# The opening in written order with halved first transfers, and a tail that scales the first row block last

## The chip, the cores and the metric

The kernel runs on one core of a Trainium2 chip. The metric is the time of one execution in microseconds of the device, the median of several runs; the profiled execution is one run more. A core has five engines that work side by side, each through its own list of instructions in order: TensorE (PE in the profile; its weight loads are PEld), VectorE (DVE), ScalarE (ACT), GpSimd (POOL) and SyncE (SP). SP, ACT and POOL also issue DMAs; an engine that issues one goes on at once, unless the issue itself has to wait for a semaphore, in which case all that stands behind it on this engine waits too.

## The reference

One decoder layer on 256 tokens of width 1024, all in float32:

```python
xn = rmsnorm(h, norm_mix_g[l])
q_a, k_a, v_a, q_b, f_b, i_b, og_b, g_a, g_b = split_cols(xn @ w_in[l])
y_a = moba_attention(q_a, k_a, v_a, positions) @ w_br_attn[l]
y_b = hgrn2(q_b, f_b, i_b, og_b, lb_all[l], hgrn_norm_g[l]) @ w_br_hgrn[l]
h = h + (sigmoid(g_a) * y_a + sigmoid(g_b) * y_b) @ w_out[l]
h = h + memory_cross_attention(rmsnorm(h, norm_x_g[l]), rmsnorm(mem, norm_mem_g[l]), ...)
hn = rmsnorm(h, norm_ffn_g[l])
gu = hn @ w_ffn_in[l]
h = h + (silu(gu[..., :2816]) * gu[..., 2816:]) @ w_ffn_out[l]
return rmsnorm(h, final_norm_g)
```

Two places matter here. The first is the product of the scaled input with the columns of `w_in` that give `f_b` (the scaling by the row's root mean square is applied later, to the product). The second is the last line: each of the 256 rows of `h` is squared and summed over its 1024 columns, the power -1/2 of the mean is taken, and the row is multiplied with it and with the gain `final_norm_g`.

## The kernel before

Every float32 product is made of three: both operands are split into a high part in the rounded type `float32r` (on ACT, L212, for the weights) and the rest (on DVE, L213), and PE adds high x high, high x low and low x high. The weights come as a row of chunks of 128 x 2048 elements (1 MB), in the order in which PE uses them, each into one of a few buffers `raw`, are split into `hi` and `lo`, and are used by PE. PE's instructions run in the order in which the code is written; ACT and DVE are otherwise ordered by a scheduler, which places each instruction where its own estimate of the times puts it, except in regions that are marked as written by hand. The kernel's DMAs from SP and ACT take eight completion semaphores (DMAHW0 to DMAHW7) in turn; a DMA whose semaphore is still in use by an earlier one waits at its issue until that one has landed.

*The opening* (L361 to L400, and L547 to L558 for PE). The tokens are held with features on the partitions, as 8 slices k of 128 features by 256 tokens. The gains and slice 0 of x are one DMA, `x0g` (L366, on ACT); slice 1 is the first `xraw` piece, slices 2 and 3 the second (both L384, on ACT), slices 4 to 7 the third (L384, on SP). `gv`, a table of all other gains and the positions, is the last DMA on ACT (L390). The first weight chunk comes in four pieces (L209, on SP, 512 columns of its 2048 each), one for each k of 0 to 3; the second chunk in two (L203), and so on. `part_x(k)` makes the high part `Xh` of a slice (slice 0 on DVE, L380, the others on ACT, L378) and the rest `Xl` (on DVE, L381). The loop of L391 takes for each k the DMA of the k-th weight piece, then `part_x(k)`, and then the split of that piece. PE first multiplies zeros (`warm`, L372, 15 matmuls of 256 columns), and then, for i of 0 to 8 (L548): four matmuls with slice i (Xh and Xl, two row blocks t, L553), and two with the low part of slice i - 1's weights (L558). `lx` and `le` (L469 to L471 on DVE) and what follows them are a small softmax over two of gv's columns; the rope tables on POOL read gv too (L407).

*The tail* (L1403 to L1468, ordered by hand on ACT, DVE, POOL and SP). The last product is added up in PSUM banks, by row block t of 128 tokens and column half c: `acc[t, c]`; block (1, 1) is finished in two quarters, `ends[0]` and `ends[1]`, with two banks of their own. For each finished piece `add_out` adds it to the residual H (DVE, L1425), `mean_part` squares it and sums the squares along the row (ACT, L1428), and `gain` multiplies it with the final gain (POOL, L1433), for all but the two quarters. `power` takes the power -1/2 of the summed mean (POOL, L1436). Row block 0 is then scaled and sent in the middle of this, half a row by ACT (L1450) and half by DVE (L1458); row block 1 at the end: half a row by ACT (L1463, sent from ACT), and the two quarters by DVE with gain and scale in one (L1467).

## Time and profile before

| | us |
|---|---|
| median of 3 runs (lowest, highest) | 600.08 (599.79, 600.6) |
| the profiled execution | 601.15 |
| its span, from the first to the last instruction | 599.4 |
| PE busy | 591.1 (99%) |
| DVE busy | 456.3 (76%) |
| ACT busy | 371.9 (62%) |
| POOL busy | 118.9 (20%) |
| mean granted clock of TensorE | 0.946 |

How to read it: times in a timeline count from the span's start. A row of the timeline gives the start, the length, the engine, the line of the code, the instruction, its output and inputs with their shapes, and in brackets how long the engine was idle before it and what ended this. An engine's name with a q (SPq, ACTq) is its instruction queue issuing a DMA. The busy time of PE counts matmuls that overlap as busy once; a busy PE is not a PE at its peak. Spans on POOL are rough.

### The profile page before, as it was taken

The numbers are of one execution on the slowest core, as the hardware profiler recorded it, in microseconds if no ns is written. First come the engines' busy times: TensorE is split into PE (matmuls) and PEld (weight loads), VectorE is DVE, ScalarE is ACT, GpSimd is POOL, SyncE is SP. The second block draws the span as 40 slices with busy tenths as digits, with TensorE's granted clock in tenths as the row PEclk, the third lists the DMA queues.
The fourth block names the chain that finished last, engine by engine and source line by source line (L and its number), as shares of the span: only waits on it lengthen the run. The fifth ranks groups of instructions, "written<-read, shape, count | busy, mean of one in ns | idle before, by whom it ended". The sixth has DMA issues, their size and how long they took to land.

```text
span 599.4 us, 8532 instructions
## 1 busy us (share of the span) xinstructions
PE 591.1 (99%) x3189; PEld 494.9 (83%) x3189; DVE 456.3 (76%) x743; ACT 371.9 (62%) x600; POOL 118.9 (20%) x137
## 2 busy tenths in 40 slices
PE   8999999999999999999999999999999999999995
PEld 7888888888888888788888888888888888888884
DVE  7689669999776866649966657787699887878763
ACT  7797464343487566637556556675488767676742
POOL 2889300212300440001312513100100000000003
PEclk9999999999999999999999999999999999999998
DMA  9959995874885579579699789765999979796501
GB/s 342 394 212 312 295 308 208 255 299 159 261 292 212 209 192 294 217 281 385 176 315 284 279 280 277 204 225 207 360 298 300 369 252 355 267 358 203 186 1 70
DMA packets 21833, 155.76 MB, mean 260 GB/s; under 512 B 2736, under 2 KB 3376, under 8 KB 5296
## 3 DMA queue, kind: packets, MB, share of 16 engines
q1 hardware_dynamic: 17712, 117.68, 51.3%
q0 software_dynamic: 2880, 20.97, 17.9%
q10 hardware_dynamic: 1200, 16.57, 7.2%
q8 instruction: 25, 0.41, 0.3%
q14 instruction: 16, 0.13, 0.1%
HBM read 154.16 MB, written 32.51 MB: 311 GB/s over the span
## 4 chain that ended last, share of the span: by engine, by line
PE 98%; DMA 1%; POOL 0%; DVE 0%; issue 0%; ACT 0%; POOLq 0%; DVEq 0%; ACTq 0%
PE pst L281 14%; PE pst L283 13%; PE pst L282 13%; PE psf L296 7%; PE bk L283 6%; PE bk L281 6%; PE bk L282 6%; PE psf L297 4%; PE acc L282 3%; PE acc L283 3%; PE acc L281 3%; PE psg L553 1%; PE pso L283 1%; PE pso L281 1%; PE pso L282 1%; PE lp L671 1%
## 5 line engine op out<-in xcount | busy, mean ns | idle before, releaser
L213 DVE TENSOR_TENSOR lo<-raw,hi 128x1024 fp32r<-128x1024 f32 (+1 forms) x128 | 156.0, 1238 | 47.6 <-ACT hi L212 45.6
L212 ACT ACTIVATE hi<-raw 128x1024 fp32r<-128x1024 f32 (+1 forms) x128 | 128.6, 1029 | 88.4 <-PE pst L283 45.2
L281 PE MATMUL pst<-hi,Xh 128*128 128x512 f32 x224 | 88.7, 396 | 0.0
L283 PE MATMUL pst<-hi,Xh 128*128 128x512 f32 x224 | 87.3, 390 | 0.0
L282 PE MATMUL pst<-lo,Xh 128*128 128x512 f32 x224 | 87.2, 389 | 0.0
L1219 DVE TENSOR_TENSOR lo<-raw,hi 128x1024 fp32r<-128x1024 f32 x56 | 66.1, 1220 | 13.9 <-ACT hi L1218 13.9
L1218 ACT ACTIVATE hi<-raw 128x1024 fp32r<-128x1024 f32 x56 | 56.3, 1053 | 21.4 <-issue 11.3
L281 PEld LDWEIGHTS pst<-hi,Xh 128*128 128x128 f32 x224 | 42.1, 188 | 9.1 <-issue 0.5
L283 PEld LDWEIGHTS pst<-hi,Xh 128*128 128x128 f32 x224 | 42.1, 188 | 8.9
L282 PEld LDWEIGHTS pst<-lo,Xh 128*128 128x128 f32 x224 | 42.1, 188 | 8.3
L1201 POOL DMA_DIRECT2D raw<-w x5 | 4.5, 895 | 119.3 <-DVE lo L1219 33.8
L281 PE MATMUL acc<-hi,hids 128*128 128x512 f32 x64 | 25.1, 392 | 0.0
L282 PE MATMUL acc<-lo,hids 128*128 128x512 f32 x64 | 24.9, 390 | 0.0
L283 PE MATMUL acc<-hi,hids 128*128 128x512 f32 x64 | 24.9, 389 | 0.0
L281 PE MATMUL bk<-hi,Sh 128*128 128x512 f32 x60 | 23.7, 396 | 0.0
L281 PE MATMUL bk<-hi,h2h 128*128 128x512 f32 x60 | 23.7, 394 | 0.0
L283 PE MATMUL bk<-hi,h2h 128*128 128x512 f32 x60 | 23.4, 390 | 0.0
L283 PE MATMUL bk<-hi,Sh 128*128 128x512 f32 x60 | 23.4, 390 | 0.0
L282 PE MATMUL bk<-lo,Sh 128*128 128x512 f32 x60 | 23.4, 389 | 0.0
L282 PE MATMUL bk<-lo,h2h 128*128 128x512 f32 x60 | 23.3, 389 | 0.0
L296 PE MATMUL psf<-H,hi 128*128 128x512 f32 x64 | 22.8, 400 | 0.0
L296 PE MATMUL psf<-M,hi 128*128 128x512 f32 x64 | 22.8, 399 | 0.0
(382 smaller groups left out, 1462.1 us busy)
## 6 DMA issues: line engine op xcount, KB each, us to landing
raw<-w SPq DMA_DIRECT2D x78, 1024.0 KB, 6.7
sum<-w POOLq DMA_DIRECT2D x15, 1024.0 KB, 12.4
raw<-sum SPq DMA_DIRECT2D x13, 1024.0 KB, 6.5
raws<-w SPq DMA_DIRECT2D x11, 1024.0 KB, 6.8
raw<-w POOLq DMA_DIRECT2D x5, 1024.0 KB, 8.6
raw<-w SPq DMA_DIRECT2D x4, 512.0 KB, 5.9
raws<-sum SPq DMA_DIRECT2D x2, 1024.0 KB, 5.1
raw<-w SPq DMA_DIRECT2D x4, 256.0 KB, 4.4
```

The source lines that it names most:

```text
L212: SC.activation(hi[:, a], raw[:, a], AF.Copy)
L213: V.tensor_tensor(lo[:, a], raw[:, a], hi[:, a].bitcast(F32), op=ALU.subtract)
L281: PE.matmul(ps, xh, h, start=first, stop=False, skip_group_check=more)
L282: PE.matmul(ps, xh, l, start=False, stop=False, skip_group_check=more)
L283: PE.matmul(ps, xl, h, start=False, stop=last, skip_group_check=more)
L296: PE.matmul(ps, w[0][:, k, a], X2[:, k], start=k == 0, stop=False)
L297: PE.matmul(ps[:, 0], w[1][:, k, a], X2[:, k, 0], start=False, stop=k == 7)
L553: PE.matmul(pss[c][t], z[:, k, t * 128:(t + 1) * 128], ws[c][0][:, k], start=z is Xh and k == 0, stop=False)
L671: PE.matmul(ps[r, j], KS[:, a, r], q, start=True, stop=True)
L1201: G.dma_start(raw_of[k], A["w"][AT_CHUNK["I", PAIRS[g][0], 1]], accum_op=ALU.add)
L1218: SC.activation(hi[:, a], raw[:, a], AF.Copy)
L1219: V.tensor_tensor(lo[:, a], raw[:, a], hi[:, a].bitcast(F32), op=ALU.subtract)
```

## The change

In the opening:

- `x0g` becomes two DMAs on ACT: slice 0's first 128 tokens with the gains, and its last 128 tokens. `Xh` and `Xl` of slice 0 are made in two halves.
- The first weight piece (512 columns) becomes two DMAs of 256 columns, each split for itself (`FIRST`), so the first chunk comes in five pieces.
- `gv` is issued on SP behind the first chunk's five pieces, and no longer on ACT.
- The opening's loop stands in a region ordered by hand for ACT and DVE, which ends after the second chunk's splits; slice 0's `part_x` comes before the first split.
- The zeros for the warm-up are written by one memset in place of memset and cast, ahead of the other two memsets, and PE makes 13 warm-up matmuls instead of 15.

In the tail:

- PE finishes `acc[1, 0]` before `acc[1, 1]`, and the two are added to H in this order.
- The gain of the first of the two last quarters is applied ahead on POOL (`gain(1, 1, 256)`).
- The last quarter's squares are summed by DVE in one instruction (`tensor_tensor_reduce`), which starts from the sum of the others; the first quarter's sum is added to that start by ACT (`Identity` with a bias).
- Row block 0 is scaled and sent only behind all of this, and not between the squares.

```diff
-WARM = 15
+WARM = 13
+FIRST = (0, 256, 512, 1024, 1536, 2048)
...
-        x0g = big("B4", "x0g", (128, 264))
-        SC.dma_start(x0g, A["x0g"])
-        zero, still = t2b("zero", (128, 256)), tb.tile([128, 256], F32R, name="still", tag="tb")
-        V.memset(zero, 0.0)
-        V.tensor_copy(still, zero)
+        x0g = [big(tag, "x0g", (128, n)) for tag, n in (("B4", 136), ("B6", 128))]
+        for i in range(2):
+            SC.dma_start(x0g[i], A["x0g%d" % i])
+        still = tb.tile([128, 256], F32R, name="still", tag="tb")
+        V.memset(still.bitcast(F32), 0.0)
+        V.memset(ones, 1.0)
+        V.memset(nhalf, -0.5)
...
+            token_halves = [(slice(128 * t, 128 * t + 128), x0g[t][:, 0:128]) for t in range(2)]
+            for a, xk in token_halves:
+                V.tensor_scalar(Xh[:, k, a], xk, g1, None, op0=ALU.mult)
+            for a, xk in token_halves:
+                V.scalar_tensor_tensor(Xl[:, k, a], xk, g1, Xh[:, k, a].bitcast(F32), op0=ALU.mult, op1=ALU.subtract)
...
-        SC.dma_start(gv, A["gv"])
-        for k in range(4):
+        region = tc.manual_schedule(engines={mybir.EngineType.Activation, mybir.EngineType.DVE})
+        region.__enter__()
+        next(opening[0])
+        part_x(0)
+        next(opening[0])
+        for k in range(1, 4):
             next(opening[0])
             part_x(k)
         run(opening[0])
+        SY.dma_start(gv, A["gv"])
         run(opening[1])
+        region.__exit__(None, None, None)
...
+        out_part(n, wb, 1, 0)
         out_part(n - 1, wa, 1, 1)
-        out_part(n, wb, 1, 0)
...
-        add_out(acc[1, 1], 1, 512, 1024)
-        V.tensor_scalar(v3[:, 0:1], ssq3[:, 0:1], ssq3[:, 1:2], EPS, op0=ALU.add, op1=ALU.add)
-        power(0, 0)
-        SC.activation(H[:, 0, 0:512], hg3[0, 0], AF.Copy, scale=rs[0])
-        send(SY, 0, 0, 512)
         add_out(acc[1, 0], 1, 0, 512)
         mean_part(2, 1, 0, 512)
         gain(1, 0)
...
+        V.tensor_scalar(v3[:, 0:1], ssq3[:, 0:1], ssq3[:, 1:2], EPS, op0=ALU.add, op1=ALU.add)
+        power(0, 0)
+        add_out(acc[1, 1], 1, 512, 1024)
+        V.tensor_scalar(v3[:, 1:2], ssq3[:, 2:3], EPS, None, op0=ALU.add)
+        add_out(ends[0], 1, 512, 768)
+        mean_part(3, 1, 512, 768)
+        gain(1, 1, 256)
+        SC.activation(v3[:, 2:3], ssq3[:, 3:4], AF.Identity, bias=v3[:, 1:2])
+        add_out(ends[1], 1, 768, 1024)
+        V.tensor_tensor_reduce(out=pt.tile([128, 256], F32, name="fjunk", tag="pt"), in0=H[:, 1, 768:1024],
+                               in1=H[:, 1, 768:1024], op0=ALU.mult, op1=ALU.add, scale=1.0 / 1024.0,
+                               scalar=v3[:, 2:3], accum_out=v3[:, 3:4])
+        power(1, 3)
+        SC.activation(H[:, 0, 0:512], hg3[0, 0], AF.Copy, scale=rs[0])
+        send(SY, 0, 0, 512)
         V.tensor_scalar(H[:, 0, 512:1024], hg3[0, 1], rs[0], None, op0=ALU.mult)
         send(SY, 0, 512, 1024)
...
+        V.tensor_scalar(H[:, 1, 512:768], hg3[1, 1][:, :256], rs[1], None, op0=ALU.mult)
+        send(SY, 1, 512, 768)
+        V.scalar_tensor_tensor(H[:, 1, 768:1024], H[:, 1, 768:1024], rs[1], gfin[:, 768:1024], op0=ALU.mult, op1=ALU.mult)
+        send(SY, 1, 768, 1024)
```

How the lists of the engines change is shown at three places. In the rows, 128x264 and the like are shapes, x4 is a count, and behind "waits" stand the semaphores that a row waits for. The first place is the start of ACT: before,

```order
L366 DMA x0g<-x0g 128x264
L387 ACT_TABLE_LOAD
L387 ACTIVATE warm_act<-ones 128x1 [waits DVE_49]
L384 DMA xraw<-xT 128x256
L384 DMA xraw<-xT 128x512
L390 DMA gv<-gv 128x90 [waits DMAHW0_49]
L212 ACTIVATE hi<-raw 128x512 [waits DMAHW1_49]
L378 ACTIVATE Xh<-xraw,x0g 128x256 [waits DMAHW4_49]
L212 ACTIVATE hi<-raw 128x512 [waits DMAHW2_49]
```

and now:

```order
L367 DMA x0g<-x0g 128x136
L367 DMA x0g<-x0g 128x128
L393 ACT_TABLE_LOAD
L393 ACTIVATE warm_act<-ones 128x1 [waits DVE_49]
L390 DMA xraw<-xT 128x256
L390 DMA xraw<-xT 128x512 [waits DMAHW0_49]
L212 ACTIVATE hi<-raw 128x256 [waits DMAHW1_49]
L212 ACTIVATE hi<-raw 128x256 [waits DMAHW3_49]
L380 ACTIVATE Xh<-xraw,x0g 128x256 [waits DMAHW6_49]
L212 ACTIVATE hi<-raw 128x512 [waits DMAHW4_49]
```

DMAHW0 is the semaphore of the first `x0g` DMA in both. The DMA of gv has gone; the second `xraw` DMA (slices 2 and 3) has the wait for DMAHW0 that gv had. On SP gv stands as the sixth DMA now, behind the five pieces of the first chunk, with a wait for DMAHW1 (the first of them) and ahead of the second chunk.

The second place is DVE in the opening, from `Xh` of slice 0 to `lo` of the weight piece for k = 2: before,

```order
L380 TENSOR_SCALAR Xh<-x0g 128x256 [waits DMAHW0_49]
L381 SCALAR_TENSOR_TENSOR Xh<-x0g,Xh 128x256 [waits DVE_49]
L213 TENSOR_TENSOR lo<-raw,hi 128x512 [waits DMAHW1_49,Activation_49]
L381 SCALAR_TENSOR_TENSOR Xh<-xraw,x0g,Xh 128x256 [waits DMAHW4_49,Activation_49]
L213 TENSOR_TENSOR lo<-raw,hi 128x512 [waits DMAHW2_49,Activation_49]
L381 SCALAR_TENSOR_TENSOR Xh<-xraw,x0g,Xh 128x256 [waits DMAHW6_49,Activation_49]
L213 TENSOR_TENSOR lo<-raw,hi 128x512 [waits DMAHW3_49,Activation_49]
```

and now (the tile Xh holds `Xh` and `Xl`; the rows L387 and L381 write `Xl`):

```order
L385 TENSOR_SCALAR Xh<-x0g 128x128 [waits DMAHW0_49]
L385 TENSOR_SCALAR Xh<-x0g 128x128 [waits DMAHW2_49]
L387 SCALAR_TENSOR_TENSOR Xh<-x0g,Xh 128x128 [waits DVE_49] x2
L213 TENSOR_TENSOR lo<-raw,hi 128x256 [waits DMAHW1_49,Activation_49]
L213 TENSOR_TENSOR lo<-raw,hi 128x256 [waits DMAHW3_49,Activation_49]
L381 SCALAR_TENSOR_TENSOR Xh<-xraw,x0g,Xh 128x256 [waits DMAHW6_49,Activation_49]
L481 TENSOR_TENSOR lx<-gv 128x8 [waits DMAHW1_49]
L213 TENSOR_TENSOR lo<-raw,hi 128x512 [waits DMAHW4_49,Activation_49]
L381 SCALAR_TENSOR_TENSOR Xh<-xraw,x0g,Xh 128x256 [waits DMAHW0_49,Activation_49]
L213 TENSOR_TENSOR lo<-raw,hi 128x512 [waits DMAHW5_49,Activation_49]
```

`lx`, which reads gv, stood behind the Xl of slices 4 to 7 before; now the scheduler has put it between `Xl` of slice 1 and `lo` of that slice's weights, into the order written by hand.

The third place is the end of DVE: before,

```order
L1425 TENSOR_TENSOR H<-acc,H 128x512 [waits PE_49] x3
L1448 TENSOR_SCALAR v_5340<-ssq_5336 128x1 [waits Activation_49]
L1425 TENSOR_TENSOR H<-acc,H 128x512 [waits PE_49]
L1425 TENSOR_TENSOR H<-bk,H 128x256 [waits DVE_49,PE_49]
L1425 TENSOR_TENSOR H<-bk,H 128x256 [waits PE_49]
L1458 TENSOR_SCALAR H<-hg_5338,r_f_5341 128x512 [waits Pool_49]
L1460 TENSOR_SCALAR v_5340<-ssq_5336 128x1 [waits Activation_49]
L1461 TENSOR_SCALAR v_5340<-ssq_5336,v_5340 128x1 [waits DVE_49,Activation_49]
L1467 SCALAR_TENSOR_TENSOR H<-H,r_f_5342,gfin 128x256 [waits Pool_49]
L1467 SCALAR_TENSOR_TENSOR H<-H,r_f_5342,gfin 128x256
```

and now (hg is a piece with its gain, r_f a power, v and ssq sums of squares; the two ISA rows are the sum of the last quarter's squares and its reading):

```order
L1437 TENSOR_TENSOR H<-acc,H 128x512 [waits PE_49] x3
L1462 TENSOR_SCALAR v_5347<-ssq_5342 128x1 [waits Activation_49]
L1437 TENSOR_TENSOR H<-acc,H 128x512 [waits PE_49]
L1465 TENSOR_SCALAR v_5347<-ssq_5342 128x1 [waits Activation_49]
L1437 TENSOR_TENSOR H<-bk,H 128x256 [waits DVE_49,PE_49]
L1437 TENSOR_TENSOR H<-bk,H 128x256 [waits PE_49]
L1471 ISA fjunk,v_5347<-H,v_5347 128x256 [waits DVE_49,Activation_49]
L1471 ISA v_5347 128x1
L1477 TENSOR_SCALAR H<-hg_5344,r_f_5348 128x512 [waits Pool_49]
L1481 TENSOR_SCALAR H<-hg_5346,r_f_5349 128x256 [waits Pool_49]
L1483 SCALAR_TENSOR_TENSOR H<-H,r_f_5349,gfin 128x256 [waits DVE_49]
```

One of the two small steps behind the last add has gone, the other stands ahead of the first quarter's add; the sum of squares has come behind the second quarter's, and row block 0's scaling stands behind it.

More of the change, by code (lines that the diff above doesn't have):

```diff
@@ L98, in lay @@
                 out[i].reshape(n, 128, 4 // n, 512)[...] = w.reshape(n, 4 // n, 128, 512).transpose(0, 2, 1, 3)
+                if i == 0:
+                    out[i].reshape(4, 2, 128, 256)[0] = w[:128].reshape(128, 2, 256).transpose(1, 0, 2)
             else:
@@ L175, in build @@
         ones = cp.tile([128, 1], F32, name="ones")
-        V.memset(nhalf, -0.5)
-        V.memset(ones, 1.0)
         ready = {}
@@ L198, in prep @@
             pieces = 4 if first else 2
-            n = 2048 // pieces
+            bounds = FIRST if i == 0 else tuple(range(0, 2049, 2048 // pieces))
             sent = PIECES[i] if i < len(PIECES) else 1
@@ L205, in prep @@
                 SY.dma_start(raw, A["w"][i])
-            for c in range(pieces):
-                a = slice(c * n, (c + 1) * n)
+            for a in (slice(*z) for z in zip(bounds, bounds[1:])):
                 if i == 0:
@@ L375, in part_x @@
         def part_x(k):
-            g1, xk = x0g[:, 256 + k:257 + k], xraw[:, k] if k else x0g[:, 0:256]
+            g1 = x0g[0][:, 128 + k:129 + k]
             if k:
-                SC.activation(Xh[:, k], xk, AF.Copy, scale=g1)
-            else:
-                V.tensor_scalar(Xh[:, k], xk, g1, None, op0=ALU.mult)
-            V.scalar_tensor_tensor(Xl[:, k], xk, g1, Xh[:, k].bitcast(F32), op0=ALU.mult, op1=ALU.subtract)
+                SC.activation(Xh[:, k], xraw[:, k], AF.Copy, scale=g1)
+                V.scalar_tensor_tensor(Xl[:, k], xraw[:, k], g1, Xh[:, k].bitcast(F32), op0=ALU.mult, op1=ALU.subtract)
+                return
+            token_halves = [(slice(128 * t, 128 * t + 128), x0g[t][:, 0:128]) for t in range(2)]
[3 more added lines that the diff above has]
+                V.scalar_tensor_tensor(Xl[:, k, a], xk, g1, Xh[:, k, a].bitcast(F32), op0=ALU.mult, op1=ALU.subtract)
         def take_x(eng, a, b):
@@ L1415, in build @@
             out_part(n, wb, 1, 1, ends[i], 256 * i, 256 * i + 256)
-        ssq3 = cp.tile([128, 5], F32, name="ssq3")
-        hg3 = {i: big(tag, "hg3", (128, 512)) for tag, i in (("B12", (0, 0)), ("B7", (0, 1)), ("B14", (1, 0)))}
-        v3 = cp.tile([128, 3], F32, name="v3")
+        ssq3 = cp.tile([128, 4], F32, name="ssq3")
+        hg3 = {i: big(tag, "hg3", (128, 512)) for tag, i in (("B12", (0, 0)), ("B7", (0, 1)), ("B14", (1, 0)), ("P1", (1, 1)))}
+        v3 = cp.tile([128, 4], F32, name="v3")
         rs = [cp.tile([128, 1], F32, name="r_f%d" % t) for t in range(2)]
@@ L1429, in mean_part, with gain @@
                           accum_out=ssq3[:, i:i + 1])
-        def gain(t, c):
-            a = slice(c * 512, (c + 1) * 512)
-            G.tensor_tensor(hg3[t, c], H[:, t, a], gfin[:, a], op=ALU.mult)
+        def gain(t, c, n=512):
+            a = slice(c * 512, c * 512 + n)
+            G.tensor_tensor(hg3[t, c][:, :n], H[:, t, a], gfin[:, a], op=ALU.mult)
         def power(t, i):
@@ L1454, in build @@
         gain(1, 0)
-        for i in range(2):
-            add_out(ends[i], 1, 512 + 256 * i, 768 + 256 * i)
-            mean_part(3 + i, 1, 512 + 256 * i, 768 + 256 * i)
+        V.tensor_scalar(v3[:, 0:1], ssq3[:, 0:1], ssq3[:, 1:2], EPS, op0=ALU.add, op1=ALU.add)
[13 more added lines that the diff above has]
+        send(SY, 0, 0, 512)
         V.tensor_scalar(H[:, 0, 512:1024], hg3[0, 1], rs[0], None, op0=ALU.mult)
         send(SY, 0, 512, 1024)
-        V.tensor_scalar(v3[:, 1:2], ssq3[:, 2:3], ssq3[:, 3:4], EPS, op0=ALU.add, op1=ALU.add)
-        V.tensor_scalar(v3[:, 2:3], ssq3[:, 4:5], v3[:, 1:2], None, op0=ALU.add)
-        power(1, 2)
         SC.activation(H[:, 1, 0:512], hg3[1, 0], AF.Copy, scale=rs[1])
         send(SC, 1, 0, 512)
-        for i in range(2):
-            a = slice(512 + 256 * i, 768 + 256 * i)
-            V.scalar_tensor_tensor(H[:, 1, a], H[:, 1, a], rs[1], gfin[:, a], op0=ALU.mult, op1=ALU.mult)
-            send(SY, 1, a.start, a.stop)
+        V.tensor_scalar(H[:, 1, 512:768], hg3[1, 1][:, :256], rs[1], None, op0=ALU.mult)
+        send(SY, 1, 512, 768)
+        V.scalar_tensor_tensor(H[:, 1, 768:1024], H[:, 1, 768:1024], rs[1], gfin[:, 768:1024], op0=ALU.mult, op1=ALU.mult)
+        send(SY, 1, 768, 1024)
         region.__exit__(None, None, None)
@@ L1494 @@
         "xT": by_piece(feats(a["x"])),
-        "x0g": np.ascontiguousarray(np.concatenate([feats(a["x"])[:, 0], cols(a["norm_mix_g"][0])], axis=1)),
+        "x0g0": np.ascontiguousarray(np.concatenate([feats(a["x"])[:, 0, :128], cols(a["norm_mix_g"][0])], axis=1)),
+        "x0g1": np.ascontiguousarray(feats(a["x"])[:, 0, 128:]),
         "xtok": tokens(a["x"]),
```

## The prediction

> **What bounds the kernel now.** I read the page first, then the windows of PE alone, then the two ends of the span. The span and the chain of work that ended last:
>
> ```profile
> span 599.4 us, 8532 instructions
> ...
> PE 98%; DMA 1%; POOL 0%; DVE 0%; issue 0%; ACT 0%; POOLq 0%; DVEq 0%; ACTq 0%
> ```
>
> The windows of PE (length, busy time with instructions, granted clock, DMA share, GB/s), first and last of four that lie end to end:
>
> ```profile
> 8.00:100.00 92.00, 92.00 (x546) 0.95 0.86 302
> ...
> 500.00:592.80 92.80, 92.80 (x427) 0.95 0.58 202
> ```
>
> In both PE is busy for the whole stretch. So the time is an opening until about 8 us, a block of matmuls without a gap, and a tail behind them. The change leaves the middle's order alone; whatever moves the last late start of the opening moves the end by as much. The chain in the opening (start, length):
>
> ```profile
> 0.73 3.51 DMA x0g<-x0g
> ...
> 4.26 0.34 ACTq L390
> 4.64 0.64 ACT hi L212
> 5.33 2.20 PE psg L553 x8
> ...
> 9.53 0.91 PE psg L553 x4
> ```
>
> The gain table's issue (L390) waits on ACT for x0g, and the first weight split stands behind it; the first real matmul is at 5.33, and one of 512 columns takes 0.227 (four in 0.91). But this is not yet the start that counts. The timeline of the opening (start, length, [idle before and its end]):
>
> ```profile
> 1.21 0.29 DVE L369 CAST still<-zero 128x256 fp32r<-128x256 f32 x1
> 1.25 0.86 ACTq L384 DMA_DIRECT2D xraw<-xT  x2
> ...
> 1.56 3.57 PE L372 MATMUL warm<-still 128*128 128x256 f32 x15 [1.56 <-DVE still L369]
> ...
> 2.56 1.80 SPq L203 DMA_DIRECT2D raw<-w  x2
> ...
> 6.79 0.51 ACT L378 ACTIVATE Xh<-xraw,x0g 128x256 fp32r<-128x256 f32 x1 [0.50 <-DMA xraw<-xT]
> ...
> 7.21 0.62 ACT L212 ACTIVATE hi<-raw 128x512 fp32r<-128x512 f32 x1
> 7.33 0.49 DVE L381 SCALAR_TENSOR_TENSOR Xh<-xraw,x0g,Xh 128x256 fp32r<-128x256 f32 x1 [0.32 <-ACT Xh L378]
> ...
> 7.86 0.69 DVE L213 TENSOR_TENSOR lo<-raw,hi 128x512 fp32r<-128x512 f32 x1
> ...
> 7.88 1.20 PE L553 MATMUL psg<-hi,Xh 128*128 128x512 f32 x4
> ```
>
> Ten matmuls from 5.33 would end at 7.6. The third feature slice (k=2) starts at 7.88, because its 256 KB of x land at 6.79, then Xh (to 7.30) and the split of the weights (to 7.83) follow on ACT. From 7.88 PE has no gap. **The start that counts is landing of xraw k=2,3 plus 1.09.**
>
> **The opening, part by part.** DMAs of the opening and, for comparison, one of the outputs (KB, us from issue to landing):
>
> ```profile
> xraw<-xT ACTq DMA_DIRECT2D x1, 256.0 KB, 5.1
> ...
> out<-H SPq DMA_DIRECT2D x2, 128.0 KB, 2.2
> ...
> x0g<-x0g ACTq DMA_DIRECT2D x1, 132.0 KB, 3.5
> ...
> gv<-gv ACTq DMA_DIRECT2D x1, 45.0 KB, 5.9
> ```
>
> *First transfers.* x0g becomes 68 and 64 KB, the first weights 128 and 128. Both x0g and raw's first piece (388 KB) are in by 4.24 now; of the first halves only 196 KB have to come. The bound below is 2.9 (0.73 plus the output row's 2.2 us), above 4.24. I take 3.85, nearer to the x0g row, since it has the same place in the queues. The second halves then come by about 4.5. With gv's issue gone from ACT, the two half splits (L212's 0.64 for 512 columns; about 0.4 each) end near 5.0, and the first real matmul starts about 0.3 earlier. Of this nothing reaches the end: the next slices wait for data.
>
> *The issue that now waits.* The order rows of ACT show that the wait for x0g (semaphore DMAHW0) has not gone; it has moved from gv to the second xraw issue, the very piece that starts k=2. Now it is issued within 1.25 to 2.11; afterwards not before 3.85, done at 4.2, with all five raw pieces of SP issued ahead of it. What that costs depends on how the two queues share the engines. Three windows of DMA, each with its total or its ACT queue (q10: packets, MB, share), for 6.0:6.5, 7.0:7.5 and 7.5:8.0:
>
> ```profile
> q10 hardware_dynamic: 4, 0.00, 1.4%
> ...
> DMA packets 53, 0.22 MB, mean 434 GB/s; under 512 B 0, under 2 KB 0, under 8 KB 53
> ...
> q10 hardware_dynamic: 13, 0.00, 3.6%
> ```
>
> gv was issued at 4.26, the ACT queue was empty from about 6.2, yet gv's first packets move after 7.5; it lands 5.9 us after its issue, with SP's raw pieces (L203, the last issued by 4.36) served first. So pieces are served about in the order of issue. In that order the second xraw piece has today 1,284 KB up to its own end (132, 256, 256, 128, 256, 256) and lands at 6.79. Afterwards SP's fourth piece (256 KB) and gv (45 KB) come in front: 301 KB more, at 434 GB/s 0.7 us. It lands at 7.5, k=2 starts at 8.6: **+0.7**. The bounds: if the queues take turns instead, it lands near where it does now, and the opening costs -0.1 to +0.4; two more small transfers in front may delay all by 0.3, so +1.0 above.
>
> The Trainium skill, "DMA: Bandwidth & Descriptors", section "Queues, rings and completion order", says that each engine takes turns between the queues packet by packet. By that rule the piece would land at about 6.9 and the opening would cost +0.4. gv's row speaks against it.
>
> *The gv wait on DVE.* In the new DVE order lx (which reads gv) stands ahead of lo of the second piece and of Xl of k=2. gv, issued on SP at about 3.8 (it waits for the first half-piece of weights) behind raw's five pieces, lands at 6.9 to 7.2 by the same count (it ends 1,329 KB). lx (0.2 as an estimate, like the small DVE step of the tail below), lo (0.69) and Xl (0.49) take 1.4 from there, to 8.6 at most, and Xl's matmuls are due at 8.6 + 2 x 0.227 = 9.05: hidden, because Xh of k=2 is late itself. If that cover goes, Xl ends at gv's landing plus 1.4, against 8.33 where it is used today. Queued behind lx is every later lo and Xl; DVE takes up lo of the second piece at 7.2 to 7.4, today 6.6 at the latest (it ends before 7.33), so it runs about 0.8 to 1.1 late from there. The next that could bind:
>
> ```profile
> 15.66 1.21 DVE L213 TENSOR_TENSOR lo<-raw,hi 128x1024 fp32r<-128x1024 f32 x1
> ```
>
> This ends at 16.9 and is used 45 matmuls after 7.88, at 18.1. Late by 0.8 to 1.1 it meets a use that is late by 0.7: it holds, and has 0.7 or more to spare.
>
> *Free edits.* The memset without the cast starts the warm-up about 0.4 earlier; two matmuls fewer; Xh and Xl of k=0 in halves on an idle DVE: nothing at the end, unless the clock minds (below).
>
> **The tail.** DVE, ACT and POOL in the timeline, and as last of these the row of the DVE reduction that the change uses anew (count, ns min/median/max):
>
> ```profile
> 592.19 0.43 DVE L1425 TENSOR_TENSOR H<-bk,H 128x256 f32<-128x256 f32 x1
> ...
> 594.05 0.21 DVE L1461 TENSOR_SCALAR v<-ssq,v 128x1 f32<-128x1 f32 x1
> ...
> 591.60 0.72 ACT L1450 ACTIVATE H<-hg,r_f 128x512 f32<-128x512 f32 x1 [1.40 <-POOL r_f L1436]
> ...
> 592.85 0.40 ACT L1428 ACTIVATE hjunk<-H 128x256 f32<-128x256 f32 x1
> 593.15 0.18 ACT L1428 ACTIVATION_READ_ACCUMULATOR hjunk<-H 128x1 f32 x1
> ...
> 594.34 0.56 POOL L1436 TENSOR_TENSOR r_f<-v,nhalf 128x1 f32<-128x1 f32 x1 [0.80 <-DVE v L1461]
> ...
> L1093 DVE CUSTOM_DVE_ANT_0 xp<-xs,rows_m x8: 412/417/419, 364.7 to 384.4; 128x256 f32<-128x256 f32 x8
> ```
>
> PE's swap brings block (1,0) 1.4 earlier and costs nothing. The quarter sum then runs: add 592.24 to 592.67 (a small DVE step stands ahead), square (0.40) from 592.72 with its read to 593.20, Identity (0.2, an estimate by L1461's 0.21) to 593.45, the reduction 593.50 to 593.92, power from 594.0 instead of 594.34: 0.34 earlier. It is paid for with the outputs. The sends, and the windows of DMA around the first and the last (length, clock, DMA share, GB/s):
>
> ```profile
> 592.35 3.90 SPq L1439 DMA_DIRECT2D out<-H  x4
> ...
> 593.00:593.50 0.50, 0.95 0.58 221
> ...
> 596.00:596.50 0.50, 0.50 0.40 133
> 596.50:597.00 0.50, 0.50 1.09 395
> ...
> 597.50:598.00 0.50, 0.50 0.51 170
> ```
>
> Today the first block's 512 KB are sent from 592.35 on and are through before the last 512 KB, which move from about 596.3 to 597.85 (the last two windows' shares). Afterwards ACT's 0.72 scaling starts only behind Identity, at 593.45, so the first send is at 594.2, its data move from 595.0 (some 0.8 behind the issue: of the send at 592.35 the 593.0 row shows the first data), and all 1,024 KB lie behind one another: at 350 to 395 GB/s 2.7 to 3.0 us, so to 597.7 to 598.0. The wait on the power is replaced by a queue of outputs: **+0.1**, with -0.2 and +0.4 as bounds.
>
> **Sum.** 599.4 + 0.7 + 0.1 = 600.2 of span. The profiled execution took 601.15 with what lies around the span, 1.07 above the median of 600.08; the difference is carried over: 600.08 + 0.8 = 600.9. A measurement of this kernel can tell about 0.2%, 1.2 us, from no change, so the forecast is no change that shows, on the slow side.
>
> **The rivals.** *The opening is even or gains* (the queues take turns, gv early): -0.1 in the opening and -0.1 in the tail give 599.9. For it: x0g and the first raw piece moved side by side; against it: gv. Chance 0.16.
>
> *gv lands as late as today, and VectorE stands for it.* If 45 KB again take 5.9 us, from 3.8, lx starts at 9.7, Xl of k=2 ends at 11.1 where it is used at 8.33 today: +2.8, with the tail 603.0, slower. It decides as soon as gv lands later than about 7.6 (9.05 less 1.4). Against it: the pieces that held gv are now issued behind it. Chance 0.10.
>
> *The clock is not released in time.* The warm-up and the tail's matmuls, same width:
>
> ```profile
> 1.56:5.10 3.54, 3.54 (x15) 1.00 0.93 289
> ...
> 591.28:592.80 1.52, 1.52 (x13) 0.95 0.00 0
> ```
>
> 0.236 apiece against 0.12: the warm-up runs at half rate throughout, and only after 3.57 us of it do matmuls of 512 columns take 0.227. Thirteen take 3.1, and then PE idles for about 0.7. If that is not enough, eight matmuls at 0.455 from 5.0 end at 8.6, two more make it 9.1, where k=2 starts at 7.88 now: +1.2, with the tail 601.4. Chance 0.14.
> The Trainium skill, "TensorE: Matmul & The Clock Gate", Part 1, gives such a rule: half clock until a window of about 3.4 us was busy. By that rule 3.1 us may fall short. The trace agrees that 3.57 us are enough; no run shows 3.1.
>
> **Chances and range.** The forecast has 0.60. Slower by over 0.2%: gv's 0.10, half of the clock's, and the forecast's upper edge (1.0 with 0.4), together 0.25. Faster by as much: no case reaches 598.9; 0.04 for what I don't see. The rest, 0.71, is the same. The range runs from 599.5 (the even case less half of the runs' spread of 0.8) to 602.0 (the clock's case with the tail's and the runs' upper ends); it leaves out gv's case.
>
> **What would show it.** Right: the second xraw issue on ACT at about 3.9, its landing near 7.5, the k=2 matmuls near 8.6, power near 594.0, and the outputs in one unbroken stretch from 595. Wrong: Xl of k=2 waiting for DVE behind lx; the first real matmuls at 0.45; k=2 before 7.9; the last output packet earlier than 597.5.

## The result, and the profile after

The changed kernel takes 604.29 us (median of 6 runs, 602.27 to 605.34) against 600.19 (6 runs, 599.79 to 601.85) for the kernel before: a ratio of 1.0062, 95% interval 1.0046 to 1.0078. It is slower by 0.6%, where 600.9 and "no change that shows" were forecast; the measured time lies above the range (599.5 to 602.0). Its runs differ by 3 us, and three of them have a lower granted clock:

| run, us | 602.27 | 603.17 (profiled) | 603.64 | 604.94 | 605.26 | 605.34 |
|---|---|---|---|---|---|---|
| granted clock | 0.997 | 0.996 | 0.995 | 0.990 | 0.990 | 0.993 |

The profiled execution has a span of 601.4. TensorE (PE) in its opening (start, length, [idle before and its end]):

```profile
1.17 3.14 PE L374 MATMUL warm<-still 128*128 128x256 f32 x13 [1.17 <-DVE nhalf L371]
4.53 1.96 PE L565 MATMUL psg<-hi,Xh 128*128 128x512 f32 x4 [0.22 <-ACT hi L212]
7.80 1.20 PE L565 MATMUL psg<-hi,Xh 128*128 128x512 f32 x4 [1.31 <-ACT hi L212]
8.84 0.63 PE L570 MATMUL psg<-lo,Xh 128*128 128x512 f32 x2
10.70 1.19 PE L565 MATMUL psg<-hi,Xh 128*128 128x512 f32 x4 [1.24 <-ACT hi L212]
```

The first real matmuls come earlier than before (4.53 against 5.33), but four of them take 1.96, where four take 1.20 further down: most of the 1.96 is at half rate. Then PE idles twice, and slice 2 (k=2), whose start counts for the end, begins at 10.70 instead of 7.88. Whom it waits for stands on ScalarE:

```profile
1.72 0.38 ACTq L390 DMA_DIRECT2D xraw<-xT  x1
3.38 0.33 ACTq L390 DMA_DIRECT2D xraw<-xT  x1
3.76 0.72 ACT L212 ACTIVATE hi<-raw 128x256 fp32r<-128x256 f32 x2 [0.61 <-DMA x0g<-x0g]
6.72 0.51 ACT L380 ACTIVATE Xh<-xraw,x0g 128x256 fp32r<-128x256 f32 x1 [2.24 <-DMA xraw<-xT]
9.62 0.51 ACT L380 ACTIVATE Xh<-xraw,x0g 128x256 fp32r<-128x256 f32 x1 [1.88 <-DMA xraw<-xT]
```

Both xraw transfers come late: the first, issued at 1.72, at 6.7; the second, issued at 3.38, at 9.6 (it landed at 6.79 before). Why shows in the windows of the DMAs (length, clock column, DMA share, GB/s):

```profile
2.50:3.00 0.50, 1.00 1.02 327
3.00:3.50 0.50, 1.00 0.84 225
3.50:4.00 0.50, 1.00 0.48 55
4.00:4.50 0.50, 1.00 0.76 287
4.50:5.00 0.50, 1.00 1.04 360
```

When the short first transfers are through, the rate falls to 55 GB/s, although the next weight piece and the first xraw have been issued since about 1.7. Before, the mean from 3 to 7 us was 380; here it is 290.

The rate is only a part of it. In the order of issue 1,585 KB (1.62 MB) come up to the end of the second xraw. The DMAs from the start to 7.5 us and from the start to 9.1 us, each with its total and with ScalarE's queue, q10 (packets, MB, share), which carries x0g and both xraw transfers, 0.53 MB:

```profile
DMA packets 1421, 1.65 MB, mean 220 GB/s; under 512 B 272, under 2 KB 912, under 8 KB 1421
q10 hardware_dynamic: 548, 0.48, 21.7%
...
DMA packets 1601, 2.25 MB, mean 247 GB/s; under 512 B 297, under 2 KB 937, under 8 KB 1601
q10 hardware_dynamic: 575, 0.53, 19.2%
```

By 7.5 us as much had moved as the order of issue asks for, but the last of xraw had not: it came only by 9.1, when 0.6 MB more had moved. By then SyncE's queue had moved 1.72 MB, where the first chunk and gv, its share ahead of xraw, are 1.09; the rest is the second weight chunk, issued at 3.87 behind xraw's 3.38. So the order of issue was not kept. In the kernel before, q10 had its 0.53 MB by 6.25 us, with 1.45 MB moved in all, near the 1.31 MB (1,284 KB) of its order.

The tail:

```profile
593.03 0.69 DVE L1437 TENSOR_TENSOR H<-acc,H 128x512 f32<-128x512 f32 x1 [0.55 <-PE acc L283]
594.89 0.29 ACT L1469 ACTIVATE v<-ssq,v 128x1 f32<-128x1 f32 x1
595.22 0.49 DVE L1471 CUSTOM_DVE_ANT_0 fjunk<-H,v 128x256 f32<-128x256 f32 x1 [0.33 <-ACT v L1469]
595.79 0.73 POOL L1448 TENSOR_TENSOR r_f<-v,nhalf 128x1 f32<-128x1 f32 x1 [0.73 <-DVE v L1471]
595.82 1.95 SPq L1451 DMA_DIRECT2D out<-H  x4
```

From the last 512-column addition (593.03) to the power it is 2.76, where it was 2.86 (591.48 to 594.34): 0.10 gained, not 0.34, and the power itself takes 0.73 instead of 0.56. The outputs are sent in one row from 595.82. From that addition to the end it is 8.37, before 7.92.

So the difference of the two profiles, +2.0 of span, is +2.8 in the opening, +0.45 in the tail and -1.3 between them. The -1.3 is no gain of the change: the profiled execution of before had a granted clock of 0.946, and its stretch from k=2 to that addition took 583.60. In the changed kernel (0.996) it takes 582.33, and in two kernels below with their clocks at 0.998 and 0.999 it takes 582.21 and 582.28. The execution that I predicted from was 1.3 long in the middle, which is why it lay 1.07 above the median; against an execution with the usual clock the change loses 3.3.

### The profile page after: what moved, and what is told of

It reads as the page before. It is cut to its first block, busy times and chain, and to the rows that moved or that the text cites. A ratio compares the mean times of both kernels' runs of the same rounds, so it can differ in the third digit from the quotient of the medians.

```text
span 601.4 us, 8535 instructions
## 1 busy us (share of the span) xinstructions
PE 590.5 (98%) x3187; PEld 494.1 (82%) x3187; DVE 455.8 (76%) x746; ACT 371.8 (62%) x600; POOL 118.0 (20%) x138
## 4 chain that ended last, share of the span: by engine, by line
PE 97%; DMA 1%; DVE 0%; ACT 0%; issue 0%; POOLq 0%; POOL 0%; DVEq 0%
PE pst L281 14%; PE pst L283 13%; PE pst L282 13%; PE psf L296 7%; PE bk L281 6%; PE bk L283 6%; PE bk L282 6%; PE psf L297 4%; PE acc L281 3%; PE acc L283 3%; PE acc L282 3%; PE pso L281 1%; PE pso L283 1%; PE pso L282 1%; PE lp L683 1%; DMA xraw<-xT 1%
## 5 line engine op out<-in xcount | busy, mean ns | idle before, releaser
L213 DVE TENSOR_TENSOR lo<-raw,hi 128x1024 fp32r<-128x1024 f32 (+2 forms) x129 | 155.7, 1228 | 46.2 <-ACT hi L212 44.3
L212 ACT ACTIVATE hi<-raw 128x1024 fp32r<-128x1024 f32 (+2 forms) x129 | 128.6, 1023 | 85.7 <-PE pst L283 51.6
L296 PE MATMUL psf<-Xh,hi 128*128 128x512 f32 x64 | 22.8, 399 | 0.0
## 6 DMA issues: line engine op xcount, KB each, us to landing
sum<-w POOLq DMA_DIRECT2D x15, 1024.0 KB, 11.4
```

The source lines that it names most:

```text
L212: SC.activation(hi[:, a], raw[:, a], AF.Copy)
L213: V.tensor_tensor(lo[:, a], raw[:, a], hi[:, a].bitcast(F32), op=ALU.subtract)
L296: PE.matmul(ps, w[0][:, k, a], X2[:, k], start=k == 0, stop=False)
```

## The experiments

The theories, by the letters that the expectations use. **A**: the loss lies in the opening; **B**: it lies in the tail. **C**: TensorE's clock is lost in the opening's idle stretches, in some runs. **D**: each DMA costs a turn whatever its size, so two more in front delay all others. **E**: the wait of the second xraw issue for x0g's semaphore does it. **F**: short first transfers let the DMAs run dry behind them, whatever their number. All runs together; the ratio's column is its interval; "rate" is the mean DMA rate from 3 to 7 us and "k=2" the start of slice 2, both of the profiled execution (those of e4, e6 and e10 are among the longest of their runs):

| kernel | us, median (lowest to highest) | ratio to before, 95% | rate, GB/s | k=2 |
|---|---|---|---|---|
| before | 600.19 | | 380 | 7.88 |
| changed | 604.29 (602.27 to 605.34) | 1.0046 to 1.0078 | 290 | 10.70 |
| e1 new opening, old tail | 603.46 (603.03 to 605.22) | 1.0047 to 1.0071 | 251 | 10.57 |
| e2 old opening, new tail | 600.53 (599.86 to 600.84) | 0.9993 to 1.0011 | 401 | 8.69 |
| e3 before, x0g in two | 600.89 (600.45 to 604.03) | 1.0007 to 1.0026 | 340 | 8.93 |
| e4 before, first weights in two | 601.03 (600.34 to 603.25) | 1.0010 to 1.0029 | 255 | 11.13 |
| e5 changed, PE kept busy | 602.67 (602.53 to 603.84) | 1.0035 to 1.0059 | 278 | 10.19 |
| e6 changed, no wait of xraw | 603.50 (602.49 to 604.77) | 1.0040 to 1.0066 | 260 | 11.72 |
| e7 changed, gv last | 605.33 (603.54 to 607.02) | 1.0067 to 1.0099 | 313 | 11.04 |
| e8 changed, first transfers whole | 599.84 (599.71 to 600.04) | 0.9986 to 1.0003 | 400 | 7.78 |
| e9 e8 with the old tail | 599.62 (599.47 to 600.02) | 0.9985 to 1.0003 | 384 | 7.68 |
| e10 e8, gv first | 601.99 (601.50 to 604.32) | 1.0026 to 1.0051 | 326 | 11.90 |
| e11 e8, 128 and 384 KB | 601.81 (601.63 to 602.07) | 1.0018 to 1.0042 | 345 | 9.59 |
| e12 e8, first weights in four | 603.16 (602.87 to 604.22) | 1.0047 to 1.0070 | 291 | 9.73 |
| e13 e10, PE kept busy | 601.15 (600.65 to 602.34) | 1.0009 to 1.0027 | 385 | 8.65 |
| e14 e11, PE kept busy | 601.36 (600.45 to 601.92) | 1.0011 to 1.0029 | 323 | 9.29 |
| e15 e9, weights ahead of tokens | 599.64 (599.20 to 600.83) | 0.9984 to 1.0002 | 393 | 8.07 |

**e1 and e2: which end.** e1 takes the old tail back (the lines below are part of it), e2 has the tail's edits alone.

```diff
-        out_part(n, wb, 1, 0)
         out_part(n - 1, wa, 1, 1)
+        out_part(n, wb, 1, 0)
...
-        V.tensor_tensor_reduce(out=pt.tile([128, 256], F32, name="fjunk", tag="pt"), in0=H[:, 1, 768:1024],
...
```

> The new opening with the old tail. Three theories of the 4.1 us (604.29 against 600.19). Theory A, the opening: in the changed kernel's trace the matmuls of slice k=2 start at 10.70 where they started at 7.88, and the outputs end 8.37 behind the last 512-column addition where they ended 7.92; so of this kernel some 0.45 less than the change's 4.1 is lost: about 603.8, k=2 again near 10.7, and the last addition to the end again 7.9. Theory B, the tail lost more than the trace of one execution shows: below 602.5. Theory C, beside A: thirteen warm-ups sometimes do not release the clock before the wait for slice 2. Then the runs of this kernel differ among each other by 2 to 3 us, with the granted clock (0.990 in the long ones, 0.997 in the short ones, as in the changed kernel's runs), while the kernel before differs by less than 1.

> The old opening with the new tail. Theory A: k=2 at 7.9 as before, and from the last 512-column addition to the end 8.4 where it was 7.92: 600.6 (+0.45). By my forecast of the tail (+0.1): 600.3. If the power at the end really came 0.3 earlier and the outputs did not queue: 599.9. Theory C: the granted clock is alike in all runs, since 15 warm-ups stand ahead.

The opening alone loses 3.2, the tail alone 0.3, which its interval doesn't tell from nothing: A holds, B falls. e1's runs differ among each other by 2.2, as C says, but their granted clocks do not follow as it says: the run of 604.39 has 0.999, the shortest, 603.03, 0.997. (From the last addition to the end it is 8.22 in e1's profile with the old tail and 8.02 in e2's with the new one: that stretch differs between executions by as much as I had put down to the tail.)

e2's slice 2 starts at 8.69, not at the 7.9 that its old opening let expect, although its second xraw was there by 6.40. PE was late by itself:

```profile
5.15 3.23 PE L553 MATMUL psg<-hi,Xh 128*128 128x512 f32 x8
```

These eight took 2.20 in the profile before. So after fifteen warm-up matmuls (3.57 us, as there) full rate does not always follow at once, which the expectation by C had taken for granted here.

**e3 and e4: one DMA more.** x0g, or the first weight piece, in two DMAs; what reads them stays whole.

```diff
-        SC.dma_start(x0g, A["x0g"])
+        for a in (slice(128, 264), slice(0, 128)):
+            SC.dma_start(x0g[:, a], A["x0g"][:, a])
```

```diff
-                    SY.dma_start(raw[:, a], piece(A["w"][i], a))
+                    for z in (slice(0, 256), slice(256, 512)):
+                        SY.dma_start(raw[:, z], piece(A["w"][i], z))
```

> The kernel before, with only the DMA of x0g split into two (columns 128 to 264, then 0 to 128) on the same queue and into the same tile; what reads it waits for both. No DMA waits for another one's semaphore that did not before, and gv stays on ScalarE's queue. Theory D, a DMA costs its turn whatever its size (in the traces the first packets of successive DMAs come some 0.55 us apart in order of issue over both queues): everything behind it is 0.5 to 0.7 later, the second xraw lands at 7.3 to 7.5 instead of 6.79, k=2 starts at 8.4 to 8.6, 600.8. Theory E, only the wait of the second xraw issue for x0g's semaphore counts, and a smaller DMA is free: k=2 at 7.9 to 8.0, 600.2. ScalarE's issue itself takes 0.4 more in either case.

> The kernel before, with only the DMA of the first weight piece split into two halves of 128 KB on SyncE's queue; the operations that read it stay whole. Theory D: one DMA more ahead of all others, k=2 at 8.4 to 8.6, 600.8; but SyncE issues the pieces behind it 0.45 later as well, while ScalarE issues its xraw pieces as early as before, so that these may overtake: at the least +0.2. Theory E: k=2 at 7.9 to 8.0, 600.2.

The two cost 0.65 and 0.8: the size that D gave for the time, and a halving is not free, as E had it. D's slice 2 misses: it starts at 8.93 in e3, not at 8.4 to 8.6. Together in the changed kernel they cost far more than 1.4, though. Three of e4's twelve runs lie at 603, and its profile is of one of those. PE there:

```profile
4.83 1.19 PE L558 MATMUL psg<-hi,Xh 128*128 128x512 f32 x4
8.40 2.08 PE L558 MATMUL psg<-hi,Xh 128*128 128x512 f32 x4 [2.38 <-ACT hi L217]
```

and the windows of PE around it (length, busy time with instructions, granted clock, DMA share, GB/s):

```profile
6.00:8.00 2.00, 0.02 (x1) 1.00 1.02 364
8.00:9.00 1.00, 0.60 (x2) 0.50 1.02 398
...
10.00:11.00 1.00, 1.00 (x4) 0.50 1.00 391
11.00:12.00 1.00, 1.00 (x5) 0.80 0.97 352
```

The first four matmuls ran at full rate (1.19); after 2.38 of idling the next four took 2.08, and the clock record shows 0.50 from 8.0 until about 11.4 (0.80 is 0.4 of the last window at half rate). A clock that had been granted was taken back for some 3.4 us. That is C, seen.

**e5: the idle stretches filled.**

```diff
-WARM = 13
+WARM = 15
...
+            for _ in range(8 if i < 2 else 0):
+                PE.matmul(warm, still[:, :128], still, start=True, stop=True)
```

> The changed kernel with TensorE kept busy in the opening: 15 warm-up matmuls instead of 13, and 8 more of them (256 columns, into the same unused bank) behind the matmuls of slice 0 and 8 behind those of slice 1, where it idled 1.31 and 1.24 us. Theory C, the clock is granted or taken back by the busy share of windows of some 3.4 us, whose place against the kernel's start differs from run to run: the idle stretches were what lost it in half of the runs (granted clock 0.990, 605 us). Then no run of this kernel is of that kind any more: all within 1 us, 602.4 to 603.4, median 602.9 where the changed kernel has 604.3. If the idle stretches had nothing to do with it: 604.3 and a spread of 3 us as before; if the added matmuls get in the way of slice 1 or 2, some 0.5 more.

602.67, and four of five runs within 0.8, the fifth at 603.84: by the medians 1.6 of the change's 4.1 was half clock (1.1 by the means, 602.98 against 604.10). With five and six runs the two intervals still overlap, so the size is rough. Its matmuls of slice 0 take 1.19 from the start, but k=2 is still at 10.19: the transfers are late on their own account. The Trainium skill, "TensorE: Matmul & The Clock Gate", Part 1, says that the clock is judged in windows of about 3.4 us that run freely, whatever the kernel does, and falls back after an idle one. The rows above agree with the length, and runs of one kernel that differ by 3 us agree with a start that differs from run to run; but here an idle stretch of 2.38 was enough.

**e6: the wait of the second xraw issue taken away** by another order of issue, with as many DMAs.

```diff
-        for i in range(2):
-            SC.dma_start(x0g[i], A["x0g%d" % i])
+        SC.dma_start(x0g[0], A["x0g0"])
...
+                if i == 0 and a.start == 0:
+                    SY.dma_start(x0g[1], A["x0g1"])
```

> The changed kernel with the second half of x0g issued by SyncE behind the first half of the first weight piece, instead of by ScalarE. As many DMAs as in the changed kernel; but the second xraw issue (slices 2 and 3) takes another semaphore and no longer waits for x0g to land: it is issued at about 1.7 to 2.1 instead of 3.38, and the last piece of the first weight chunk waits in its place. If that wait is the larger part of the loss (theory E): xraw lands at 7.5 to 8 instead of 9.6, k=2 at 8.6 to 9.2, the shorter runs at 601.3 to 602 and the median not above 602.5. If only the number of DMAs counts (theory D alone), k=2 stays near 10.7 and the time at 603 to 604.

E's times miss: 603.5 where it had at most 602.5. xraw's second piece is there in time now, but another transfer is late instead, the second half of the first weights:

```profile
0.73 0.38 SPq L209 DMA_DIRECT2D raw<-w  x1
...
1.64 1.96 SPq L209 DMA_DIRECT2D raw<-w  x4
...
3.08 0.42 ACT L214 ACTIVATE hi<-raw 128x256 fp32r<-128x256 f32 x1 [0.41 <-DMA raw<-w]
6.82 0.42 ACT L214 ACTIVATE hi<-raw 128x256 fp32r<-128x256 f32 x1 [3.33 <-DMA raw<-w]
```

128 KB, issued at 1.64, are waited for until 6.82; the 128 KB issued ahead of them at 0.73 came by 3.08. This edit also puts x0g's second half ahead of them on SyncE's queue, so it moves the delay and does not take the wait away alone; that the wait is not needed for a loss show e3 and e4, which have none. PE's first matmul starts at 7.29 here, the ten of slices 0 and 1 run at half rate, and slice 2 follows at 11.72.

**e7: gv last.**

```diff
-        SY.dma_start(gv, A["gv"])
         run(opening[1])
...
             take_x(SY, *piece_x)
+        SY.dma_start(gv, A["gv"])
```

> The changed kernel with gv issued behind the last xraw piece on SyncE instead of ahead of the second weight chunk. Theory D: xraw's second piece has one DMA fewer ahead of it, 0.5 earlier, k=2 near 10.2, 602.7 in the shorter runs; and lx no longer holds VectorE. If what lies ahead of xraw by bytes counts, the second weight chunk (1,024 KB, issued 0.4 earlier) overtakes it instead, and k=2 stays or comes later: 603.2 to 604.5. If gv and lx do nothing, as I forecast: 603.2 in the shorter runs, 604.3 in the median.

605.33, a microsecond worse than the change by the medians, with intervals that overlap. gv and lx are not what costs. xraw's second piece is waited for until 9.96, which fits the second weight chunk, issued at 3.04 instead of 3.87, getting ahead of it.

**e8: the first transfers whole again,** all else as changed.

```diff
-FIRST = (0, 256, 512, 1024, 1536, 2048)
+FIRST = (0, 512, 1024, 1536, 2048)
...
-        for i in range(2):
-            SC.dma_start(x0g[i], A["x0g%d" % i])
+        SC.dma_start(x0g, A["x0g"])
```

> The changed kernel with x0g and the first weight piece in one DMA each again (and slice 0 split in one operation for the weights), the rest as changed: order by hand, gv on SyncE, 13 warm-ups, new tail. No xraw issue waits any more and two DMAs fewer stand in front. Theories D and E alike: k=2 at 7.9 to 8.4, 600.2 + 0.3 of tail = 600.5 in the shorter runs; with theory C some runs 1 to 2 us longer, since 13 warm-ups end at 4.3 and the first weights come at 4.6. If the order by hand or gv on SyncE cost by themselves: above 602.

This edit takes back the whole loss: 599.84, all runs within 0.33. It undoes both halvings at once, and with them the wait of the second xraw issue. Its windows of DMA and the rows that answer to those above:

```profile
3.00:3.50 0.50, 1.00 1.08 396
3.50:4.00 0.50, 1.00 1.02 387
4.00:4.50 0.50, 1.00 1.10 402
```

```profile
6.44 0.51 ACT L377 ACTIVATE Xh<-xraw,x0g 128x256 fp32r<-128x256 f32 x1 [0.23 <-DMA xraw<-xT]
```

No slump, xraw's second piece at 6.44, and PE runs without a gap from 4.56. The order by hand, gv on SyncE and thirteen warm-ups together cost nothing. Against this kernel the changed one's profile is 3.3 longer: 2.92 in the opening (10.70 less 7.78), 0.12 between, 0.26 in the tail.

**e9: e8 with the old tail** (the edit of e1).

> The kernel of the last experiment (new order by hand, gv on SyncE, 13 warm-ups, x0g and the first weight piece whole: 599.84 us, 599.71 to 600.04) with the old tail. It isolates the tail where runs differ by 0.3 only. By the trace of the changed kernel (8.37 against 7.92 from the last 512-column addition to the end) the new tail costs 0.45, so 599.4 here; by my forecast of +0.1, 599.7; if the new tail gains, above 599.84.

599.62, and 0.45 below the runs of before beside it, where e8 was 0.42 below its own: the new tail costs between 0.03 and 0.22, which these runs do not tell from nothing. In the profiles, from the last addition to the end, it is 8.11 in e8 and 7.84 here.

**e10 to e12: number against size.** gv in front of x0g; pieces of 128 and 384 KB; the first weights in four.

```diff
+        SC.dma_start(gv, A["gv"])
         SC.dma_start(x0g, A["x0g"])
```

```diff
-                if i == 0:
-                    SY.dma_start(raw[:, a], piece(A["w"][i], a))
+                if i == 0 and a.start != 512:
+                    z = slice(256, 1024) if a.start == 256 else a
+                    SY.dma_start(raw[:, z], piece(A["w"][i], z))
```

```diff
+                if i == 0 and a.start == 0:
+                    for z in (slice(128 * q, 128 * q + 128) for q in range(4)):
+                        SY.dma_start(raw[:, z], piece(A["w"][i], z))
```

> The same kernel (599.84) with gv (45 KB) issued by ScalarE ahead of x0g instead of by SyncE behind the first weight chunk: one DMA more in front of the first ones, nothing halved, no wait added. Theory D, a DMA costs its turn whatever its size: all later ones 0.5 to 0.6 later, k=2 at 8.3 to 8.4 where it was 7.78, 600.4. If bytes count, 45 KB are 0.1: k=2 at 7.9, 599.9 to 600.0.

> The same kernel (599.84) with the first weight piece of 128 KB and the second of 384 KB, so as many DMAs and bytes as there. Theory D: the number decides, k=2 at 7.8 to 7.9, 599.8 to 600.1, and no slump of the DMA rate at 3.2 to 4.2 us. Theory F, a first transfer that is short lets the data run dry behind it, whatever the number: the slump (33 to 120 GB/s for 0.75 us in the changed kernel) comes here too, k=2 0.5 to 1 later, 600.4 to 601.

> The same kernel (599.84) with the first weight piece in four DMAs of 64 KB on SyncE: three more DMAs in front, the same bytes; pieces three and four of the chunk now wait for semaphores of the first ones. Theory D: the four quarters come 0.5 to 0.6 apart, in a plateau of some 120 GB/s beside x0g, the second piece starts at 4 instead of 3.27, k=2 at 9.3 to 9.8, 601.3 to 601.9 (more where the clock is lost in the wait). Theory F and bytes alone: the plateau would be absent, k=2 at 7.8 to 8.3, 600 to 600.4.

All three miss D's numbers: 2.15 for one DMA more, 2.0 for none more, 3.3 for three more. F's slump is not in e11 either (287 GB/s or more from 2.5 us on); it is in e12 (115 to 152 GB/s from 3.25 to 4.0). Since PE idled 0.9 to 2.3 in each, half clock could hold the rest.

**e13 and e14: e10 and e11 with PE kept busy** (`WARM = 18` and 4 more behind slice 0; `WARM = 21`).

```diff
-WARM = 13
+WARM = 21
```

> The kernel with gv issued first (601.99, 601.5 to 604.3, against 599.84 without), with 18 warm-up matmuls instead of 13 and 4 more behind those of slice 0, so that TensorE hardly idles ahead of slice 2. Theories C and D together: one DMA more costs 0.5 to 0.7, the other 1.4 of the 2.1 were half clock, since 13 warm-ups ended 0.93 ahead of the first matmuls; then 600.4 to 600.8, all runs within 1 us. If the transfers themselves come 2 us later (xraw's first piece landed at 8.09 in that profile), 601.5 to 602 as before.

> The kernel with pieces of 128 and 384 KB (601.81), with 21 warm-up matmuls instead of 13: its first matmuls waited until 5.73 for the second half of the weights of slice 0, which came with the 384 KB, and it ran at half clock until 8.89. Theories C and D: as many DMAs as in the kernel of 599.84, so with the clock granted only the later landing is left: the matmuls of slices 0 and 1 run 2.2 from 5.75, lo 0.5, k=2 at 8.4 to 8.5 instead of 7.78: 600.4 to 600.6. Theory F: 601.5 to 601.9 as before.

601.15 and 601.36, both above what C and D together gave (600.4 to 600.8, 600.4 to 600.6): by the medians the clock's share was 0.8 and 0.45, less than I had put down to it, and the second is within the intervals. What is left, 1.3 and 1.5 over e8, is later landing. In e14's profile it is the second xraw again, issued at about 1.7:

```profile
8.21 0.51 ACT L382 ACTIVATE Xh<-xraw,x0g 128x256 fp32r<-128x256 f32 x1 [2.09 <-DMA xraw<-xT]
```

with as many DMAs and bytes in front as in e8, where it was there at 6.44. The rates from 3 to 7 us, e14 and then e8:

```profile
3.00:7.00 4.00, 1.00 0.99 323
```

```profile
3.00:7.00 4.00, 1.00 1.07 400
```

The order is not kept here either. The DMAs of e14 up to 7.75 us and of e8 up to 6.0 us, by when q10 has its 0.53 MB:

```profile
DMA packets 1196, 1.89 MB, mean 243 GB/s; under 512 B 235, under 2 KB 619, under 8 KB 1196
q10 hardware_dynamic: 431, 0.53, 22.0%
...
DMA packets 940, 1.47 MB, mean 245 GB/s; under 512 B 96, under 2 KB 352, under 8 KB 940
q10 hardware_dynamic: 432, 0.53, 24.6%
```

The mean up to then is the same; e14's second xraw is late because 0.4 MB more has moved ahead of its end. So D is not the whole: a turn per DMA would leave e14 at 600.4 to 600.6. The Trainium skill, "Perfetto Trace Analysis", "DMA Instruction — HWDGE (DVE, Sync)", has a generator of descriptors that the issuing engines share and lock for one DMA at a time, which is a turn of D's kind; e3 and e4 agree with it, e14 shows that it is not all. By the table, with 256 KB of weights and 132 KB of x0g first the DMAs move 380 to 401 GB/s from 3 to 7 us (before, e2, e8, e9, e15), and in every kernel that splits or shortens one of these 251 to 345; with gv ahead of whole ones it is 326 in e10 and 385 in e13, the same DMAs in two executions. **Why the rate falls and the order is lost stays open**: no view shows what the DMA engines wait for. Nor was the number of DMAs told from the size of their packets: every split here is by columns, so it shortens the packets too (from 2 to 3 us 375 packets for 0.28 MB in the changed kernel, 138 for 0.23 MB in e8), and no run splits by partitions.

**e15: an attempt at less than e9.**

```diff
                 SC.activation(hi[:, a], raw[:, a], AF.Copy)
+                if i == 0:
+                    yield
                 V.tensor_tensor(lo[:, a], raw[:, a], hi[:, a].bitcast(F32), op=ALU.subtract)
...
-        for k in range(1, 4):
-            next(opening[0])
-            part_x(k)
-        run(opening[0])
+        for k in range(4):
+            next(opening[0])
+            if k:
+                part_x(k)
+            next(opening[0], None)
```

> An attempt to beat both kernels: the kernel of 599.62 (order by hand, gv on SyncE, first transfers whole, old tail) with the weights of slices 1 to 3 split ahead of the tokens on ScalarE (hi, then Xh; VectorE keeps Xl ahead of lo). In the profile of its fellow (599.84) ScalarE waited 0.68 and 0.23 for xraw while the weights had landed. Up to 0.3 earlier at k=2 (7.5 instead of 7.78): 599.3 to 599.5; no change, 599.6, if TensorE, which ran slices 0 and 1 without a gap there, is what sets k=2; 599.8 if Xl, now up to 0.24 later, is waited for.

599.64, as e9: the second case of the three. e8, e9 and e15 are the lowest of all, 0.4 to 0.5 below the kernel before, and each interval just reaches 1.

## Why the prediction was wrong

- **PE without a gap from k=2, and the end moves with it**: right. From k=2 to the last addition the changed kernel takes 582.33, e8 582.21, e9 582.28.
- **The first halves**: x0g's first half came earlier than forecast (by 3.38, when the xraw issue that waits for it starts; forecast 3.85, bounds 2.9 and 4.24), the first matmuls at 4.53 (forecast 5.0). Hidden, as said, and worth nothing.
- **"lands 7.5 by issue-order byte count", opening +0.7: here it failed.** Wrong was not the issue (3.38, forecast 3.85 or later) but both halves of the count: that the bytes in front would flow at 434 GB/s without a break, and that "pieces are served about in the order of issue". Behind halved transfers the rate fell to 55 and averaged 290 from 3 to 7 us, so that the 1,585 KB of the count had moved by about 7.5; and then 0.6 MB more went before xraw's last packets, of a weight chunk issued after it. xraw landed at 9.6 and k=2 began at 10.70: +2.8 to +2.9 where the upper bound was +1.0. As an estimate, 0.6 of the 2.1 between the forecast landing and the measured one is rate and 1.5 is order: before, 0.54 passed from 6.25, when q10 had its bytes, to 6.79, and 7.5 plus as much is 8.1. I had concluded the order from gv's late packets alone and had set the sharing of the engines by turns aside with it. I had seen the danger ("two more small transfers in front may delay all by 0.3") and priced it from transfers alone. One such split costs 0.65 or 0.8 (e3, e4); both, in the changed kernel against e8, 3.3 in the profiles and 4.45 in the medians.
- **The wait behind x0g's semaphore**, which I took as the cause of the +0.7, is not shown to be decisive: without it, in another order of issue, the time is 603.5 (e6), and e3 and e4 lose time with no such wait.
- **gv and lx**: gv landed later than I said: lx, which waits for it, runs at 8.16 (forecast 6.9 to 7.2, decisive from 7.6). It held nothing up, since xraw was later still; with gv out of the way the time is no better (e7). That rival's 603.0 is near the measured time by another mechanism.

```profile
8.16 0.17 DVE L481 TENSOR_TENSOR lx<-gv 128x8 f32<-128x8 f32 x1 [0.42 <-DMA gv<-gv]
```

- **The clock not released in time** (0.14, 601.4): half right. That 3.57 us of warm-up are enough held in the trace before and not in e2's, so the number of warm-ups does not settle it. Thirteen cost nothing in e8, where little idling follows; behind the late transfers PE idles, and the clock is lost in some runs. By e5, which has both more warm-ups and the stretches filled, it is worth some 1.6 in the median. I priced it as an alternative to the late landing, and it came on top.
- **Tail +0.1**: right in size (0.03 to 0.22 by e8 and e9; neither they nor e2 can tell it from nothing). The power gained 0.10 instead of 0.34, and the outputs follow in one row as forecast.
- **The sum** was carried over from an execution with a granted clock of 0.946, 1.07 above the median. That did not spoil the forecast, a difference, but it hides 1.3 of the loss when the two profiles are compared.
- **The signs named in advance**: of those for right only the unbroken outputs came; of those for wrong the first matmuls at half rate (four in 1.96), which in that execution were hidden. A slump of the DMA rate was not on the list.

## What to carry to other kernels

Splitting the first transfers buys an early start of work that waits for the later transfers anyway; look first at which landing sets the start that counts, and at whether the DMAs still run at their full rate, and still serve that landing ahead of what is issued after it, behind the split. Where PE waits in the opening, keep it busy until the last late operand is there, because an idle stretch can cost a second time in the clock, and in some runs only: look at the spread of the runs as well as at the median. Before two profiles are compared, compare their granted clocks and the stretch that the change leaves alone.
